# Output projection of a two-layer encoder: four leading first-half products, the gated product kept in PSUM, three residual rows, and the first half's forms in three stages

## The chip, the cores and the metric

The kernel runs on one core of one Trainium2 chip. The metric is the device time of one execution in microseconds (us); the time of a kernel is the median of several runs. The engines are named as in the profile: PE (TensorE, matmuls and transposes), ACT (ScalarE), DVE (VectorE), POOL (GpSimd) and SP (SyncE, which issues all DMA transfers of this kernel). The granted clock is the share of TensorE's full clock that the throttle let through.

## The reference

The reference is one inference step of a streaming encoder with two layers, for 1024 prompt tokens and 128 sample tokens (8 sequences of 16), at a width of 1024. Each layer has an attention mixer and a gated feed-forward block with a short causal convolution. What matters here is the end of the mixer and the start of the feed-forward block:

```
mix = o @ w_o                                    # o: attention output
x = layer_norm(alpha * x + (1 + g_m) * mix, ln_g, ln_b)
h = x * (1 + sc_f) + sh_f                        # affine by c, per group
f, conv_rows = conv_ffn(h, prev, w_up, conv_w, conv_b, w_down)
```

Layer 0 attends over a sliding window, layer 1 over a wider chunk band with a shared key/value projection. All arithmetic is float32. The kernel gets it on PE by splitting each operand into a high part of a shorter format and the low rest: three matmuls (low x high, high x low, high x high) make one product.

## The kernel before, in words

The 1152 tokens are nine tiles of 128; tiles 0 to 7 are the prompt, tile 8 is the sample group. A framework lays the instructions out: the program is traced in Python order, and a planner with its own model of durations then decides, when the kernel is built, in which order each engine issues its instructions. Every engine works its own order off strictly; data dependencies become semaphore waits. `issue_after(ins)` ties the instructions of a block behind a given one on that one's engine. Buffers are columns of a few large SBUF tensors (F with 11040 columns, HX, X1, wh/wl for split weights, ws for raw ones), cut by hand; two uses of the same columns order each other.

`attention` walks through 16 heads (pairs `c`, `a` of chunk and half) with four groups of queries each, and weaves the sample group's items into them. The normalised output of each half head (`normalise`, L709 to 720: c, a and the half h of the tokens) lies in `on` (F columns) and goes to DRAM, from where it is read back chunk by chunk, split, and put into HX (`oload`); the last chunk (c = 7) is split directly into HX, in two halves of 512 tokens. The sample group's output goes through the DRAM tensor oSD.

`out_proj` (L1013) follows, once per layer. It loads the output weights in eight pieces (L1019), four for the first 512 output columns (w0) and four for the last 512 (w1); the places of w1's last two pieces are free only when the attention's last values are done. A product (`half`, L1036; matmuls at L395) is 24 matmuls of 512 columns into one PSUM bank, from a ring of four banks. DVE multiplies it by the gate (L1041) into a temporary in F, and adds ALPHA times the residual row (L1042). After both halves of a tile `norm_tail` (L967) computes the statistics, normalises (L970), lets PE transpose the tile (L976) into banks of a second ring of four, and lets ACT (L988, or DVE at L1005 for the sample tile) apply the affine into a place `hb[HOME[t]]`; the row is stored to xd (L996). The order of the tiles is ORD. The first two and the last two go as pairs (both first halves, then both second halves), the five between one by one. The residual rows (`residual`, L1010) come into a ring of two buffers.

The feed-forward block multiplies 2 x 2 blocks with seven products instead of eight, so it needs seven sums of blocks, here called forms (P1 to P7), of both its operands. `forms` (L1131) makes them for the tokens, in two halves of the tokens (q = 0 and 1), each in three parts i (two tiles' first halves, the sample tile's share, the second halves): three or four subtractions and seven splits (ACT casts at L165, POOL or DVE subtracts at L176). For q = 0 they run on POOL, for q = 1 on DVE. `prep` (L1081) does the same for the weights, on ACT and POOL. `up_phase` (L1171) starts with `unit(0, (0,))` (matmuls at L1196): block 0 of the weights times the first half of the tokens, into banks 0 to 2; its intermediate copies (L1214) and sums (L1217) lie in the columns of F that `out_proj` used.

Around the change, the columns of F hold, before: the sample keys and values of the attention (0 to 2176), `on` (2176 to 3200), sample tables, the block-diagonal queries `qbd` (3744 to 5792); and in `out_proj` the sample gate (0 to 1024), the product's temporary (1024 to 2048), the prompt gate (2048 to 3072), and the two residual buffers (3072 to 5120).

Of the kernel before, what the change touches and what calls it, by code (L numbers as in the profile page):

```python
# [13 lines left out]
ALU = mybir.AluOpType  # L14
# [7 lines left out]
ALPHA = 4.0 ** 0.25  # L22
# [19 lines left out]
ITEMS = [24 + 3 * k for k in range(8)] + [51 + (3 * k) // 2 for k in range(8)]  # L42
VA = ()
BIG = 1e30
ORD = (0, 2, 8, 1, 3, 4, 6, 5, 7)
HOME = {0: 0, 8: 1, 2: 2, 1: 3, 3: 4, 4: 0, 6: 2, 5: 3, 7: 4}
GRP = ((0, 1, 2), (3, 4, 5), (6, 7, 8))
P1, P2, P6, P5, P7, P4, P3 = range(7)
# [6 lines left out]
class Ring:  # L55
# [4 lines left out]
    def next(self):  # L60
        r = self.items[self.i % len(self.items)]
        self.i += 1
        return r
# [30 lines left out]
class Trunk:  # L94
# [361 lines left out]
    def attention(self, l, wk):  # L456
        nc, I = self.nc, self.I
# [23 lines left out]
        fa = Arena(self.F)  # L481
        sKt = fa.take(2176)
        sV = ga.take(1536)
        on = fa.take(1024)
        sb = fa.ring(2, 272)
        sK = Ring([sKt[:, 0:1088], sKt[:, 1088:2176]])
        qbd = fa.take(2048).rearrange("p (c s a q) -> p c s a q", c=8, s=8, a=2)
        pall = fa.take(NP[l] * W)
        pring = Ring([pall[:, i * W : (i + 1) * W] for i in range(NP[l])])
        bias = fa.ring(2, W)  # L490
# [18 lines left out]
        nc.gpsimd.memset(qbd[0:64, :, :, 1, :], 0.0)  # L509
        nc.gpsimd.memset(qbd[64:128, :, :, 0, :], 0.0)  # L510

        def head_of(c, a):
            return 8 * (c // 4) + 4 * a + c % 4 if l == 0 else 2 * c + a
# [19 lines left out]
        else:  # L533
# [8 lines left out]
            qload(0)  # L542
            self.load_hm(Ring([pall[:, i * 1024 : i * 1024 + 1024] for i in range(3)]), self.affine(4, (8, 9), 1))

        if l == 0:
            self.wring = Ring(self.wslots[0:2])
        sbt = []
# [161 lines left out]
        def normalise(c, a, h):  # L709
            r = slice(64 * a, 64 * a + 64)  # L710
            q = slice(h * 512, h * 512 + 512)
            src = self.rD[l][2 * c + a : 2 * c + a + 1, q]
            st = nc.sync.dma_start(rb[r, :], bass.AP(src.tensor, src.offset, [[0, 64], [1, 512]]))
# [300 lines left out]
    def out_proj(self, l, xsrc, xdst, aff):  # L1014
        nc, I, H = self.nc, self.I, self.H
        wo = I[("wo0", "wo1")[l]]
        X1 = self.X1
        loc = ((5120, 6144), (7168, 8192), (0, 2048), (3072, 1024))
        loc = [tuple(X1[:, o : o + 1024] for o in p) for p in loc]  # L1019
        loc = self.wslots[0:2] + loc + [self.wslots[2], (X1[:, 4096:5120], self.wslots[3][1])]  # L1020
        w = [self.wload(wo[i // 4, i % 4], el="ppppvvvv"[i], dst=d) for i, d in enumerate(loc)]
        w0, w1 = w[0:4], w[4:8]
        F = self.F
        self.G = self.x2p.tile([128, 2304], F32R, name=f"gup{l}", tag="x2b")
        self.gateS, tmp, self.gateP = (F[:, i * 1024 : i * 1024 + 1024] for i in range(3))
# [9 lines left out]
        def half(t, x, hf):  # L1035
            ps = self.bank(mb.next())  # L1036
            self.mmX(ps, t * 128, (w0, w1)[hf], 2, 512)
            cs = slice(hf * 512, hf * 512 + 512)
            gate = self.gateP if t < 8 else self.gateS
            v = tr.next()  # L1040
            nc.vector.tensor_mul(v, ps, gate[:, cs])  # L1041
            st = nc.vector.scalar_tensor_tensor(x[:, cs], x[:, cs], ALPHA, v, op0=ALU.mult, op1=ALU.add)  # L1042
            self.lasthalf = st.ins

        def pair(ts, between=None):
            xs = [(t, self.residual(t, xsrc, xring)) for t in ts]
            for t, x in xs:
                half(t, x, 0)
            if between:
                between()  # L1050
            for t, x in xs:
                half(t, x, 1)
                self.norm_tail(t, x, xdst, aff, tb, hb[HOME[t]])

        HX = self.HX
        pair(ORD[0:2])
        for t in ORD[2:7]:
            if t == 8:
                s3 = hb[HOME[8]]
                nc.sync.dma_start(s3, self.oSD.rearrange("c p t -> p c t"))  # L1060
                self.split(s3, H[:, t, 0], H[:, t, 1], "a", "v")
            x = self.residual(t, xsrc, xring)
            half(t, x, 0)
            half(t, x, 1)
            self.norm_tail(t, x, xdst, aff, tb, hb[HOME[t]])
# [11 lines left out]
        pair(ORD[7:], lambda: self.first.extend(self.first.pop()()))  # L1077
        self.fring = Ring(self.fslots[3:8] + [self.fslots[0], self.fslots[8]] + self.fslots[1:3])
        self.late = [self.forms(1, hb, "v", i) for i in range(3)]

    def prep(self, l, j, n=7):  # L1081
        raw = []
# [50 lines left out]
    def forms(self, q, hb, e, i):  # L1133
# [17 lines left out]
        put(P2, b21)  # L1151
        with ExitStack() as es:
            if q:
                es.enter_context(self.tc.issue_after(self.lasthalf))
            put(P3, b22)
            E.tensor_sub(b11, b12, b11)
            E.tensor_sub(b12, b22, b12)
            E.tensor_sub(b22, b22, b11)
            E.tensor_sub(b21, b21, b22)
            put(P6, b22)  # L1160

        def rest():
            put(P5, b11)
            put(P7, b12)
            put(P4, b21)

        return rest

    def ffn(self, l, xsrc, xdst, affs):
        self.up_phase(l)  # L1170
# [2 lines left out]
    def up_phase(self, l):  # L1173
# [112 lines left out]

        unit(0, (0,), self.first)
        for f in self.late:
            f()
        w1 = prep(1)  # L1290
        unit(1, (0,), w1)
        for p in U:
# [317 lines left out]
```

## Time and profile before

| | us |
|---|---|
| runs shown | 2827.95, 2832.05, 2833.47 |
| median | 2832.05 |
| profiled execution | 2830.41 |
| its span, first to last instruction | 2828.6 |
| attention, out_proj and the start of the up phase, layer 0 | about 110 to 545 |
| the same, layer 1 | about 1560 to 2096 |

The mean granted TensorE clock of the profiled execution was 0.986. In the span's 40 slices PE is busy nine tenths in nearly all. Times in the profile are counted from the span's first instruction. A row of a timeline reads: start, duration, engine, line, operation, output<-input, shapes and count, and in square brackets how long the engine stood idle before it and what ended that. A row of stretches reads: start:end, length, busy time with the number of instructions, granted clock, busy share of the DMA engines, GB/s.

### The profile page before, as it was taken

What the parts mean: (1) busy time and instruction counts of PE and PEld (TensorE: products, weight loads), DVE (VectorE), ACT (ScalarE), POOL (GpSimd) and SP (SyncE); (2) the same over time, 40 slices, a digit from 0 to 9 for tenths busy, and PEclk for the clock granted to TensorE, in tenths of its full rate; (3) what the DMA queues carried; (4) which work ended last, traced back from release to release, by engine and by line L of the source; (5) the groups of instructions that cost most, each with busy time, mean ns of one, the idle gap of its engine ahead of it and who ended that gap; (6) DMA issues with size and microseconds to landing.
All of it is one profiled execution on the core that took longest, in us unless ns stands there. A gap on an engine that the chain in (4) does not pass through costs nothing.

```text
span 2828.6 us, 48878 instructions
## 1 busy us (share of the span) xinstructions
PE 2710.7 (96%) x18086; PEld 2423.8 (86%) x18086; DVE 1664.5 (59%) x3830; ACT 1409.2 (50%) x3012; POOL 1064.3 (38%) x1086
## 2 busy tenths in 40 slices
PE   8999889999999999999999999988999999999998
PEld 6987768899999998888998888866799999998886
DVE  4466656755555566766213677774766555567764
ACT  3565644554444444545425666662455545555441
POOL 1122337775566530001541121231877666640000
PEclk9999999999999999999999999999999999999999
DMA  8655343244433447865975457683222222239661
GB/s 327 193 154 170 113 131 116 92 139 140 145 131 132 151 157 266 309 216 183 308 236 183 112 146 188 171 248 99 98 89 79 71 74 81 78 101 296 228 208 72
DMA packets 215870, 454.47 MB, mean 161 GB/s; under 512 B 39280, under 2 KB 115264, under 8 KB 215632
## 3 DMA queue, kind: packets, MB, share of 16 engines
q1 hardware_dynamic: 215632, 451.35, 49.5%
q8 instruction: 143, 2.34, 0.3%
q14 instruction: 95, 0.78, 0.1%
HBM read 359.40 MB, written 101.30 MB: 163 GB/s over the span
## 4 chain that ended last, share of the span: by engine, by line
PE 76%; DMA 7%; DVE 7%; issue 4%; ACT 3%; POOL 3%; SPq 0%; POOLq 0%; DVEq 0%; ACTq 0%
PE PS L1196 33%; PE PS L1347 16%; PE PS L383 11%; PE PS L395 5%; PE PS L679 2%; DMA F<-in_adaw_dram 2%; PE PS L660 2%; PE PS L318 2%; PE PS L634 1%; POOL HX L176 1%; PE PS L637 1%; DVE F L600 1%; DMA ws<-in_wo_dram 1%; ACT HX L165 1%; DMA ws<-oN 1%
## 5 line engine op out<-in xcount | busy, mean ns | idle before, releaser
L176 POOL TENSOR_TENSOR wl<-ws,wh 128x512 fp32r<-128x512 f32 (+1 forms) x217 | 324.5, 1498 | 653.2 <-ACT wh L165 629.5
L1250 DVE SCALAR_TENSOR_TENSOR PS<-F,PS 128x512 f32<-128x512 f32 (+2 forms) x704 | 348.7, 516 | 145.8 <-ACT PS L1257 61.0
L1196 PE MATMUL PS<-HX,wh 128*128 128x288 f32 x2616 | 401.8, 297 | 0.0
L165 ACT CAST wh<-ws 128x512 fp32r<-128x512 f32 (+1 forms) x321 | 244.8, 768 | 315.1 <-PE PS L1347 94.4
L1196 PEld LDWEIGHTS PS<-HX,wh 128*128 128x128 f32 x2616 | 365.2, 189 | 8.1 <-issue 7.4
L1347 PE MATMUL PS<-wh,HX 128*128 128x512 f32 x1164 | 362.1, 390 | 0.8 <-DVE HX L176 0.8
L1196 PE MATMUL PS<-HX,wl 128*128 128x288 f32 x1536 | 254.1, 297 | 7.0 <-DVE F L1217 4.7
L1347 PEld LDWEIGHTS PS<-wh,HX 128*128 128x128 f32 x1164 | 218.5, 188 | 46.0 <-DVE HX L176 1.3
L383 PE MATMUL PS<-HX,wh 128*128 128x384 f32 x1248 | 245.7, 340 | 0.0
L1196 PEld LDWEIGHTS PS<-HX,wl 128*128 128x128 f32 x1536 | 220.0, 189 | 14.4 <-issue 10.4
L1347 PE MATMUL PS<-wl,HX 128*128 128x512 f32 x582 | 226.9, 390 | 0.6 <-DVE wl L176 0.6
L383 PEld LDWEIGHTS PS<-HX,wh 128*128 128x128 f32 x1248 | 217.0, 189 | 5.4 <-issue 2.7
L395 PE MATMUL PS<-wh,HX 128*128 128x256 f32 (+1 forms) x936 | 173.5, 316 | 19.3 <-ACT wh L165 8.8
L1196 PE MATMUL PS<-x1att,wh 128*128 128x288 f32 x1168 | 182.1, 298 | 0.0
L1257 ACT ACTIVATE PS<-F 128x512 f32<-128x512 f32 x176 | 138.1, 785 | 77.5 <-DVE F L1229 63.2
L165 ACT CAST HX<-F 128x384 fp32r<-128x384 f32 (+3 forms) x232 | 135.9, 603 | 68.8 <-PE PS L1347 11.5
L1196 PEld LDWEIGHTS PS<-x1att,wh 128*128 128x128 f32 x1168 | 164.5, 189 | 4.9 <-issue 4.9
L716 POOL TENSOR_TENSOR F<-F,gatt 64x512 f32<-64x512 f32 x62 | 79.5, 1282 | 227.9 <-DVE F L691 201.2
L395 PEld LDWEIGHTS PS<-wh,HX 128*128 128x128 f32 x936 | 137.4, 195 | 30.6 <-ACT wh L165 9.3
L176 DVE TENSOR_TENSOR HX<-F,HX 128x384 fp32r<-128x384 f32 (+2 forms) x188 | 133.5, 719 | 41.3 <-ACT HX L165 40.1
L1347 PE MATMUL PS<-HX 128*128 128x512 f32 x630 | 145.1, 389 | 0.0
L383 PE MATMUL PS<-HX,wl 128*128 128x384 f32 x624 | 130.7, 349 | 9.6 <-DVE HX L167 4.4
(244 smaller groups left out, 5495.8 us busy)
## 6 DMA issues: line engine op xcount, KB each, us to landing
F<-in_adaw_dram SPq DMA_DIRECT2D x112, 512.0 KB
ws<-in_wup_dram SPq DMA_DIRECT2D x92, 512.0 KB
ws<-in_wdn_dram SPq DMA_DIRECT2D x88, 512.0 KB
actD<-F SPq DMA_DIRECT2D x44, 576.0 KB
F<-actD SPq DMA_DIRECT2D x132, 192.0 KB
F<-in_wdn_dram SPq DMA_DIRECT2D x44, 512.0 KB
x1att<-kH SPq DMA_DIRECT2D x60, 256.0 KB
xd<-F SPq DMA_DIRECT2D x27, 512.0 KB
```

The costliest lines, as they stand in the source:

```text
L165: self.lastact = nc.scalar.copy(out, in_).ins
L176: self.eng(el).tensor_sub(lo, src, hi.bitcast(F32))
L318: mm = nc.tensor.matmul(ps[32 * j : 32 * j + 32, hf * 256 : hf * 256 + 256], self.cT[:, k * 32 : k * 32 + 32], w[n][:, j * 256 : j * 256 + ...
L383: self.nc.tensor.matmul(out, w[a][:, k * 128 : k * 128 + 128], self.Hx(p, k, s0, n), start=i == 0, stop=i == 23)
L395: self.nc.tensor.matmul(out[:, 0:n], H[:, t0 // 128, p, j * kn + k, :], w[a][:, k * n : k * n + n], start=i == 0, stop=i == 23,)
L660: nc.tensor.transpose(t[:, m * 128 : m * 128 + 128], p[:, (kt - k0) * 128 : (kt - k0) * 128 + 128], self.ident)
L679: nc.tensor.matmul(ob[:, i0 * 128 : i0 * 128 + w], vst[a][:, kt, :], pp[:, m1 : m1 + w], start=cnt == 0, stop=cnt == 2 * len(order) - 1, s ...
L716: self.eng("v" if last else "p").tensor_mul(on[r, q], on[r, q], rb[r, :])
L1196: nc.tensor.matmul(out, w[f][a][:, k * 128 : k * 128 + 128], x[:, k, :], start=start and i == 0, stop=i == 11, skip_group_check=True,)
L1250: nc.vector.scalar_tensor_tensor(o, v, w(i), o, op0=ALU.mult, op1=ALU.add)
L1257: nc.scalar.activation(yp, u[:, bl, 2:258], AF.Identity, bias=w(3), scale=w(2))
L1347: nc.tensor.matmul(ps, h[p][:, i * 128 : i * 128 + 128], w[q][:, hf * 512 : hf * 512 + 512], start=j == 0 and k == 0, stop=j == NFF - 1 an ...
```

## The change: what it does

- `attention`: in F, `on` moves behind `qbd`, so that `sb` lies at 2176, `qbd` at 2720 and `on` at 4768. The two memsets of `qbd` are traced later, after the key and value projections. The DMA that fetches the reciprocal sums for the half head (7, 1, 0), the last of tokens 0 to 511, is remembered as `earlydma`.
- `out_proj`: the prompt gate lies at 0 to 1024, the sample gate at 4096 to 5120, three residual buffers at 1024 to 4096. The prompt gate and the first three residual rows are issued behind `earlydma`, the sample gate behind the last such DMA, as is the load of the sample tile.
- The order of the tiles is 0, 2, 1, 3, 8, 4, 6, 5, 7 instead of 0, 2, 8, 1, 3, 4, 6, 5, 7. The first-half products of tiles 0, 2, 1 and 3 come first; then each of the four gets its add, its second half and its norm in turn. The last two tiles stay a pair.
- The multiply by the gate writes the product's own PSUM bank, the add reads it there; the temporary is gone. Products have five banks (0 to 4), transposes three (5 to 7).
- `forms` becomes a generator. For q = 0 and two full tiles it has three stages: P1, P3 and three subtractions; P5 and P7; P2, the fourth subtraction, P6 and P4. The first stage of part 0 is traced after the second tile, that of part 2 after the fourth, then the second stage of both; after the sample tile, now the fifth, come its part and all the rest. For q = 1 the operations and their order stay.

The diff, cut to its core:

```diff
-ORD = (0, 2, 8, 1, 3, 4, 6, 5, 7)
+ORD = (0, 2, 1, 3, 8, 4, 6, 5, 7)
...
-        on = fa.take(1024)
         sb = fa.ring(2, 272)
         sK = Ring([sKt[:, 0:1088], sKt[:, 1088:2176]])
         qbd = fa.take(2048).rearrange("p (c s a q) -> p c s a q", c=8, s=8, a=2)
+        on = fa.take(1024)
...
+            if (c, a, h) == (7, 1, 0):
+                self.earlydma = st.ins
...
-        self.gateS, tmp, self.gateP = (F[:, i * 1024 : i * 1024 + 1024] for i in range(3))
-        xring = Ring([F[:, 4096:5120], F[:, 3072:4096]])
+        self.gateP, self.gateS = (F[:, o : o + 1024] for o in (0, 4096))
+        xring = Ring([F[:, i * 1024 : i * 1024 + 1024] for i in (1, 2, 3)])
...
+        with self.tc.issue_after(self.earlydma):
+            self.ln_gate(l, 0, False)
+            xs = [self.residual(t, xsrc, xring) for t in ORD[0:3]]
         with self.tc.issue_after(self.lastdma):
-            self.ln_gate(l, 0, False)
             self.ln_gate(l, 0, True)
-        mb = Ring([0, 1, 2, 3])
-        tb = Ring([4, 5, 6, 7])
-        tr = Ring([tmp[:, 0:512], tmp[:, 512:1024]])
+        mb = Ring([0, 1, 2, 3, 4])
+        tb = Ring([5, 6, 7])
...
-            v = tr.next()
-            nc.vector.tensor_mul(v, ps, gate[:, cs])
-            st = nc.vector.scalar_tensor_tensor(x[:, cs], x[:, cs], ALPHA, v, op0=ALU.mult, op1=ALU.add)
+            nc.vector.tensor_mul(ps, ps, gate[:, cs])
+            st = nc.vector.scalar_tensor_tensor(x[:, cs], x[:, cs], ALPHA, ps, op0=ALU.mult, op1=ALU.add)
...
-        pair(ORD[0:2])
-        for t in ORD[2:7]:
+        ps = [product(t, 0) for t in ORD[0:4]]
+        for n, t in enumerate(ORD[0:4]):
+            x = xs[n] if n < 3 else self.residual(t, xsrc, xring)
+            add(t, x, 0, ps[n])
+            half(t, x, 1)
+            norm(t, x)
+            if n == 1:
+                parts = [self.forms(0, hb, "p", 0)]
+                next(parts[0])
+            elif n == 3:
+                parts.append(self.forms(0, hb, "p", 2))
+                next(parts[1])
+                for f in parts:
+                    next(f)
+        for t in ORD[4:7]:
             if t == 8:
                 s3 = hb[HOME[8]]
-                nc.sync.dma_start(s3, self.oSD.rearrange("c p t -> p c t"))
+                with self.tc.issue_after(self.lastdma):
+                    nc.sync.dma_start(s3, self.oSD.rearrange("c p t -> p c t"))
                 self.split(s3, H[:, t, 0], H[:, t, 1], "a", "v")
...
             if t == 8:
-                rest = [self.forms(0, hb, "p", i) for i in (0, 1)]
-            elif t == 3:
-                rest.append(self.forms(0, hb, "p", 2))
-                for f in rest:
-                    f()
+                parts.append(self.forms(0, hb, "p", 1))
+                next(parts[2])
+                for f in parts:
+                    list(f)
```

More of the change, by code (lines that the diff above doesn't have):

```diff
@@ L507, in attention @@
         kH, kS, vH, vS = self.kH[l], self.kS[l], self.vH[l], self.vS[l]
-        nc.gpsimd.memset(qbd[0:64, :, :, 1, :], 0.0)
-        nc.gpsimd.memset(qbd[64:128, :, :, 0, :], 0.0)
         def head_of(c, a):
@@ L543, in attention @@
             self.load_hm(Ring([pall[:, i * 1024 : i * 1024 + 1024] for i in range(3)]), self.affine(4, (8, 9), 1))
+        nc.gpsimd.memset(qbd[0:64, :, :, 1, :], 0.0)
+        nc.gpsimd.memset(qbd[64:128, :, :, 0, :], 0.0)
         if l == 0:
@@ L1028, in out_proj, with product, add @@
         with self.tc.issue_after(self.lastdma):
-            self.ln_gate(l, 0, False)
             self.ln_gate(l, 0, True)
-        mb = Ring([0, 1, 2, 3])
-        tb = Ring([4, 5, 6, 7])
-        tr = Ring([tmp[:, 0:512], tmp[:, 512:1024]])
-        def half(t, x, hf):
+        mb = Ring([0, 1, 2, 3, 4])
+        tb = Ring([5, 6, 7])
+        def product(t, hf):
             ps = self.bank(mb.next())
             self.mmX(ps, t * 128, (w0, w1)[hf], 2, 512)
+            return ps
+        def add(t, x, hf, ps):
@@ L1038, in half @@
             cs = slice(hf * 512, hf * 512 + 512)
             gate = self.gateP if t < 8 else self.gateS
-            v = tr.next()
-            nc.vector.tensor_mul(v, ps, gate[:, cs])
-            st = nc.vector.scalar_tensor_tensor(x[:, cs], x[:, cs], ALPHA, v, op0=ALU.mult, op1=ALU.add)
+            nc.vector.tensor_mul(ps, ps, gate[:, cs])
+            st = nc.vector.scalar_tensor_tensor(x[:, cs], x[:, cs], ALPHA, ps, op0=ALU.mult, op1=ALU.add)
             self.lasthalf = st.ins
[L1045 to L1053, printed above, removed]
@@ L1055, in out_proj, with half, norm @@
-        HX = self.HX
-        pair(ORD[0:2])
-        for t in ORD[2:7]:
+        def half(t, x, hf):
+            add(t, x, hf, product(t, hf))
+        def norm(t, x):
+            self.norm_tail(t, x, xdst, aff, tb, hb[HOME[t]])
+        HX = self.HX
+        ps = [product(t, 0) for t in ORD[0:4]]
[12 more added lines that the diff above has]
+                    next(f)
@@ L1064, in out_proj @@
             half(t, x, 1)
-            self.norm_tail(t, x, xdst, aff, tb, hb[HOME[t]])
+            norm(t, x)
             if t == 8:
-                rest = [self.forms(0, hb, "p", i) for i in (0, 1)]
-            elif t == 3:
-                rest.append(self.forms(0, hb, "p", 2))
-                for f in rest:
-                    f()
+                parts.append(self.forms(0, hb, "p", 1))
+                next(parts[2])
+                for f in parts:
+                    list(f)
         first = [self.fslots[8], self.fslots[0]]
@@ L1076, in out_proj @@
         self.first = self.prep(l, 0, 5)
-        pair(ORD[7:], lambda: self.first.extend(self.first.pop()()))
+        xs = [(t, self.residual(t, xsrc, xring)) for t in ORD[7:]]
+        for t, x in xs:
+            half(t, x, 0)
+        self.first.extend(self.first.pop()())
+        for t, x in xs:
+            half(t, x, 1)
+            norm(t, x)
         self.fring = Ring(self.fslots[3:8] + [self.fslots[0], self.fslots[8]] + self.fslots[1:3])
         self.late = [self.forms(1, hb, "v", i) for i in range(3)]
+        for f in self.late:
+            next(f)
     def prep(self, l, j, n=7):
@@ L1150, in forms @@
         put(P1, b11)
-        put(P2, b21)
+        if q:
+            put(P2, b21)
         with ExitStack() as es:
@@ L1158, in forms @@
             E.tensor_sub(b22, b22, b11)
+            if q:
+                E.tensor_sub(b21, b21, b22)
+                put(P6, b22)
+        yield
+        if q == 0 and i != 1:
+            put(P5, b11)
+            put(P7, b12)
+            yield
+        if q == 0:
+            put(P2, b21)
             E.tensor_sub(b21, b21, b22)
             put(P6, b22)
-        def rest():
+        if q or i == 1:
             put(P5, b11)
             put(P7, b12)
-            put(P4, b21)
-        return rest
+        put(P4, b21)
     def ffn(self, l, xsrc, xdst, affs):
@@ L1288, in up_phase @@
         for f in self.late:
-            f()
+            list(f)
         w1 = prep(1)
```

## The prediction

> **What bounds the kernel now.** I read the page's first part first: how busy TensorE (PE) is.
>
> ```profile
> span 2828.6 us, 48878 instructions
> PE 2710.7 (96%) x18086; PEld 2423.8 (86%) x18086; DVE 1664.5 (59%) x3830; ACT 1409.2 (50%) x3012; POOL 1064.3 (38%) x1086
> ```
>
> PE is busy 96% of the span, so an edit pays only where PE stands still or runs at a lower granted clock. Next I read the two output projections in stretches (columns: PE busy and its count, granted clock, DMA share, GB/s), cut at the long waits that PE's timeline shows there.
>
> ```profile
> 404.00:417.28 13.28, 8.75 (x25) 0.74 0.53 177
> 417.28:501.65 84.37, 84.27 (x393) 1.00 0.29 101
> 501.65:515.11 13.46, 9.13 (x57) 0.87 0.22 78
> 515.11:530.00 14.89, 13.46 (x97) 1.00 0.21 72
> 1934.15:1952.55 18.40, 8.34 (x25) 0.80 0.48 142
> 1952.55:2039.42 86.87, 85.63 (x392) 0.98 0.28 98
> 2039.42:2053.43 14.01, 7.60 (x57) 1.00 0.19 75
> 2053.43:2068.00 14.57, 14.01 (x91) 0.88 0.19 73
> ```
>
> Rows 2 and 6 are the long middle of the projection in layers 0 and 1: PE has no gap to give there. Rows 1 and 5, the **front**, are what follows the attention; rows 3 and 7, the **seam**, what follows the last product. PE's timeline names the waits:
>
> ```profile
> 406.32 2.07 PE L395 MATMUL PS<-wh,HX 128*128 128x512 f32 x4 [2.36 <-ACT wh L165]
> 417.28 0.73 PE L395 MATMUL PS<-wh,HX 128*128 128x512 f32 x2 [1.81 <-DVE F L1041]
> 457.25 5.77 PE L395 MATMUL PS<-x1att,HX 128*128 128x512 f32 x24
> 462.85 0.63 PE L395 MATMUL PS<-wh,HX 128*128 128x512 f32 x2
> 507.50 1.25 PE L976 MATMUL PS<-C,F 128*128 128x128 f32 x8 [2.78 <-DVE F L970]
> 1939.76 2.08 PE L395 MATMUL PS<-wh,HX 128*128 128x512 f32 x4 [5.60 <-ACT wh L165]
> 1952.55 1.22 PE L395 MATMUL PS<-wh,HX 128*128 128x512 f32 x2 [4.45 <-DVE F L1041]
> 1988.83 1.06 PE L976 MATMUL PS<-C,F 128*128 128x128 f32 x8 [1.24 <-DVE F L970]
> 2045.80 1.06 PE L976 MATMUL PS<-C,F 128*128 128x128 f32 x8 [3.30 <-DVE F L970]
> 2053.43 0.77 PE L1196 MATMUL PS<-HX,wl 128*128 128x288 f32 x4 [3.11 <-DVE F L1217]
> ```
>
> A product is 24 matmuls and four are open (banks 0 to 3). The third row to the fourth gives the full rate: 24 in 5.60 us, 0.233 us each. At the front the first wait is for late weights (w1, the second half's columns), the second for a bank whose product stands there until the gate comes:
>
> ```profile
> 410.50 0.33 SPq L920 DMA_DIRECT2D F<-gd x1
> 404.01 1.04 ACT L165 CAST HX<-F 128x1024 fp32r<-128x1024 f32 x1 [2.60 <-DMA F<-oSD]
> 408.65 1.22 DVE L176 TENSOR_TENSOR wl<-ws,x1att 128x1024 fp32r<-128x1024 f32 x1
> 409.79 0.69 DVE L176 TENSOR_TENSOR HX<-F,HX 128x512 fp32r<-128x512 f32 x1
> 416.53 1.29 DVE L1041 TENSOR_TENSOR F<-PS,F 128x512 f32<-128x512 f32 x2 [6.05 <-DMA F<-gd]
> 1941.63 1.23 DVE L176 TENSOR_TENSOR wl<-ws,x1att 128x1024 fp32r<-128x1024 f32 x1
> ```
>
> ACT stood behind the sample tile's load before it could cast w1; the last low part of w1 was there at 409.87 and 1942.86. The prompt gate could only be loaded at 410.50, when the attention output `on` had been read for the last time (409.79 + 0.69), because both lie in the same columns of F; it took 6.0 us.
>
> **The change part by part.** *Four leading products and a fifth bank.* In the stretch 404.00 to 417.28, 24 matmuls ran; at 0.233 us they are 5.6 us, so 7.7 of 13.28 us are lost, to waits and a halved clock (first row; the second is used below):
>
> ```profile
> 406.00:408.00 2.00, 1.68 (x4) 0.50 0.02 6
> 1907.00:1934.20 27.20, 24.78 (x165) 0.94 0.32 90
> ```
>
> Layer 1 loses 18.40 - 5.6 = 12.8 us, and its middle is 86.87 - 84.37 = 2.5 us longer than layer 0's for the same work, of which 1.24 is the wait of the row at 1988.83 and 1.3 a restart at half clock. The front thus holds 7.7 + 12.8 + 1.3 = 21.8 us. Does the change reach all of it? Before, 72 matmuls could run without the late w1 parts: 2 tiles x 24 with w0, and 2 x 12 with the first two parts of w1. Now it is 4 x 24 + 12 = 108: the four tiles hold tokens 0 to 511, which need nothing of the last half head. The 36 more are 8.4 us of work from 404.0 and 1934.15 on, to 412.4 and 1942.6, and the 12 that then follow on bank 4 need the third part first. So the weights (409.87, 1942.86) are in time even if ACT still stands behind the sample tile. If the planner spends some of the 36 in gaps before, that gap is filled instead: no loss.
>
> [...]
>
> *Gate and three residual rows early.* The prompt gate now lies over the sample keys, free when the last sample scores are done, and is issued behind the half head before the last, and the rows too:
>
> ```profile
> 362.99 0.45 PE L763 MATMUL PS<-F 128*32 128x144 f32 x8
> 393.52 0.42 PE L798 MATMUL PS<-F 16*32 16x128 f32 x8
> 381.24 0.45 SPq L713 DMA_DIRECT2D gatt<-rD x1
> 1901.63 0.45 SPq L713 DMA_DIRECT2D gatt<-rD x1
> ```
>
> In layer 0 the gate can go at about 382 and lands near 388; a row may go from 394 (the last read of the sample's new values). In layer 1 all go behind 1901.6. At 6.0 us a load, the gate and the first row are in by 400 in layer 0 and 1914 in layer 1, the other rows 12 us later; bank 0 is wanted when t0's second product is done, 412.4 + 2.8 = 415. On SP they may stand ahead of the last loads of w_o; the price, if these slip by all four loads (24 us), is a rival below. The sample gate goes last, for tile 8, now fifth, some 40 us later: nothing. DVE gets the first four gated adds earlier: 8 operations of about 0.68 us, 5.4 us, where it idled 6.05 us for the gate. Nothing queued behind them is due before w1, so nothing.
>
> *Product stays in PSUM.* The multiply writes its bank, and the add reads it. The bank is held one add longer; five banks at 5.6 us a product cover that.
>
> ```profile
> L1041 DVE TENSOR_TENSOR F<-PS,F x36: 669/679/694, 416.5 to 2045.6; 128x512 f32<-128x512 f32 x36
> L1042 DVE SCALAR_TENSOR_TENSOR F<-F x36: 670/770/1830, 417.7 to 2046.3; 128x512 f32<-128x512 f32 x36
> ```
>
> No PSUM output of this form is shown, so its multiply lies between 0.67 us (the present one) and 1.8 (the worst add); I take 0.68. DVE has room at 11 us of PE per tile: nothing on the path; at the upper end 18 x 1.1 = 20 us of DVE per layer would still fit outside the seam, and cost it up to 2 us. The add reads PSUM for one operand and should stay near 0.68. [...]
>
> *Order, forms in stages, third residual buffer.* Here the seam's rows (timelines of POOL, SP and DVE, two of the chain):
>
> ```profile
> 487.71 2.99 POOL L176 TENSOR_TENSOR wl<-ws,wh 128x512 fp32r<-128x512 f32 x2
> 491.16 0.37 SPq L1010 DMA_DIRECT2D F<-in_xrow_dram x1
> 496.52 0.69 DVE L1042 SCALAR_TENSOR_TENSOR F<-F 128x512 f32<-128x512 f32 x1 [4.34 <-DMA F<-in_xrow_dram]
> 2024.33 4.74 DMA xd<-F
> 796.49 12.78 PE PS L1196 x96
> ```
>
> The same casts and subtractions run on ACT, DVE and POOL. POOL's first weights for the next phase were ready at 490.7, 11 us before PE's last product (501.65); its first forms now start one tile earlier, so this cover shrinks little as PE comes sooner. The memsets only move behind other POOL work of the attention's start, long before the items that read them: nothing.
>
> Today the last row (tile 7) waits for its buffer's store, behind POOL's weights on SP; DVE waits 4.34 us for it, tile 5's norm slides, and PE stands in order at tile 5's transposes (2.78 and 3.30 us). With three buffers the row is there a tile earlier. In rows 3 and 7 of the stretches PE did 48 unit matmuls (12.78/96 = 0.133 us, 6.4 us) and 8 transposes, 0.85 us (row 2: 84.37 less 336 x 0.2333, over seven tiles): 7.2 us. Lost: 6.2 and 6.8, together 13.0 us. What is late next: the first unit copies to columns 2320 to 2896 of F, which now are tile 5's buffer, so it waits for tile 5's store. Before, DVE went on at 496.52 and reached tile 5's transposes at 507.50, 11.0 us. Tile 5's last product now ends 5.6 us before PE's last; with the same 11.0 and 4.7 for the store the copy could start 10.1 us behind the last product. PE covers P1, P2, P5 (36 x 0.133) and the transposes, 5.6 us, so the wait is 4.5 us at most and 0 at least. I take 1.5, nearer to nothing: the 11.0 us held tile 7's add and forms that now go ahead of it. The seam gives 13.0 - 3.0 = 10.0 us.
>
> **Sum.** 21.8 + 10.0 = 31.8 us. The profiled execution took 2830.4 us (its span 2828.6 and 1.8 around it), so 2798.6; the median of the three runs shown is 1.6 us above it: 2800 us.
>
> **The rivals.**
> (1) *The seam stays as long*: the store of tile 5, or DVE's late forms, take the place of the row. For it: DVE is nearly full there. Against: 4.34 us of DVE waiting goes. Front only: 2832 - 21.8 = 2810.
> (2) *The gate isn't early*: SP's order puts the rows, which wait for the last sample read, or the loads of w_o in the way. If w1 comes 24 us later, at 434, PE stands in layer 0 from 412.4 to 434; it had the same 108 matmuls done at 417.28 + 2.8 = 420.1, so it is 14 us worse there. Layer 1, with 40 us from 1901.6 to 1941.6, still gains its 14.1. If the seam stays long too, that is no change, 2832. Against: SP's order is laid out by readiness, and the DMA queues stand half idle (shares 0.53 and 0.48).
> (3) *Slower: ACT holds the transposes' banks.* They have three banks instead of four; ACT takes casts and affines in one order, and a cast waits for POOL's subtractions:
>
> ```profile
> ACT HX L165 <- POOL F L1158: 3.5, 2, 2.1
> ```
>
> The leading tiles come 6.4 us apart (5.6 and 0.85 of transposes), and a tile needs the bank that the tile before gave first, so it decides from about 3.5 us of ACT waiting per tile. If six tiles a layer each stop PE for 3.5 us, that is 42 us against 31.8: 2842. Against: the longest such wait is 2.1 us.
> (4) *More*: the stretches after the seam held 89 and 83 unit matmuls and 8 transposes, 12.7 and 11.9 us, in 14.89 and 14.57: 4.9 us. With the 3.0 of the store, the 1.24 at 1988.83 and the 2.4 us of gaps from 1907 to 1934 filled as well, 43.3 us: 2789.
>
> **How the numbers follow.** Forecast 0.58, (1) 0.18, (2) 0.07, (3) 0.07, (4) 0.10. The range reaches from just under (4), 2788, past (1) to half the front and no seam, 2832 - 10.9 = 2821, so 2822. Measured here, less than 0.2% (5.7 us) can't be told from no change. Faster: forecast, (1) and (4), 0.86; same: 0.07; slower: 0.07.
>
> **What would show it.** In the profile after: no PE wait over 1 us between the attention's last matmul and the first transposes, granted clock 1.00 there; the gate's load issued before `on` is read; DVE's add never above 0.8 us; the last residual row issued before the product that uses it; PE's first wait behind the last product under 3 us. It is wrong if PE waits at a transpose for ACT, if ACT's copy of the first unit waits many us for a store, or if the front's waits stand with other releasers.

## The result, and the profile after

The kernel after takes 2802.4 us (median of six runs, 2797.2 to 2810.2) against 2829.1 for the kernel before in the same session: ratio 0.9907, 95% interval 0.9896 to 0.9919. Its profiled execution took 2800.65 us, 29.8 less than the one before. The page and PE's stretches, cut as before (columns as in the prediction):

```profile
span 2798.5 us, 48858 instructions
...
PE 2700.2 (96%) x18086; PEld 2415.9 (86%) x18086; DVE 1665.2 (60%) x3830; ACT 1408.9 (50%) x3012; POOL 1056.7 (38%) x1086
```

```profile
406.15:493.01 86.86, 86.26 (x401) 1.00 0.35 117
493.01:501.78 8.77, 6.13 (x46) 1.00 0.35 120
501.78:506.50 4.72, 4.72 (x24) 0.65 0.03 8
...
1921.70:2009.50 87.80, 85.39 (x400) 0.98 0.32 110
2009.50:2018.45 8.95, 5.82 (x45) 1.00 0.14 59
2018.45:2030.40 11.95, 9.13 (x48) 0.71 0.21 66
```

Behind the attention PE now goes straight through the products: the front's lost time is gone (first and fourth row; the fourth keeps one wait, at the first transposes). The seam still loses time in three ways: idle time (second and fifth row), the half clock that follows it (third and sixth: 0.65 and 0.71 on average, 0.50 from 504.0 to 506.5 and from 2021.0 to 2024.0), and more waits after that. PE's timeline after names them:

```profile
1997.50 1.32 PE L977 MATMUL PS<-C,F 128*128 128x128 f32 x8 [2.41 <-DVE F L971]
...
501.78 2.09 PE L1225 MATMUL PS<-HX 128*128 128x288 f32 x12 [2.63 <-ACT F L1243]
...
2018.45 1.13 PE L1225 MATMUL PS<-HX 128*128 128x288 f32 x4 [3.13 <-ACT F L1243]
2021.09 1.33 PE L1225 MATMUL PS<-x1att,wl 128*128 128x288 f32 x4 [1.50 <-ACT x1att L165]
2027.93 1.34 PE L1225 MATMUL PS<-x1att,wh 128*128 128x288 f32 x8 [1.08 <-DVE C L933]
```

Lines have moved: products are still L395, the norm is L971, the transposes L977, the unit's matmuls L1225 and its first copy L1243. The transposes of tile 5, which waited 2.78 and 3.30 us before, are in none of these rows: they no longer stop PE.

To follow the gain I compare four points of PE's timeline in the two traces: the first unit matmul (end of the front), the last one of the up phase, and the projection matmul (L383) with which layer 1 goes on after layer 0's feed-forward block.

| | before | after | gain in the part |
|---|---|---|---|
| layer 0, first unit matmul | 501.65 | 493.01 | 8.6 |
| layer 0, last unit matmul | 1054.60 | 1042.62 | 3.3 |
| layer 1, projection matmul | 1542.99 | 1530.96 | 0.1 |
| layer 1, first unit matmul | 2039.42 | 2009.53 | 17.9 |
| layer 1, last unit matmul | 2544.32 | 2514.70 | -0.3 |
| end of the span | 2828.6 | 2798.5 | 0.5 |

So the fronts, each with the attention ahead of it, gave 26.5 us and the up phases, seams included, 3.1. The total is the predicted one; its two terms are not.

### The profile page after: what moved, and what is told of

The parts are those of the page before. It is cut to its first block, busy times and chain, and to the rows that moved or that the text cites. A ratio compares the mean times of both kernels' runs of the same rounds, so it can differ in the third digit from the quotient of the medians.

```text
span 2798.5 us, 48858 instructions
## 1 busy us (share of the span) xinstructions
PE 2700.2 (96%) x18086; PEld 2415.9 (86%) x18086; DVE 1665.2 (60%) x3830; ACT 1408.9 (50%) x3012; POOL 1056.7 (38%) x1086
## 4 chain that ended last, share of the span: by engine, by line
PE 77%; DVE 8%; DMA 7%; issue 4%; ACT 3%; POOL 1%; SPq 1%; POOLq 0%; ACTq 0%; DVEq 0%
PE PS L1225 34%; PE PS L1376 17%; PE PS L383 9%; PE PS L395 7%; DMA F<-in_adaw_dram 3%; PE PS L678 2%; PE PS L318 2%; PE PS L659 2%; PE PS L633 1%; DMA ws<-in_wo_dram 1%; DVE F L599 1%; PE PS L636 1%; DVE x1att L176 1%; PE PS L977 1%; PE PS L799 1%
## 5 line engine op out<-in xcount | busy, mean ns | idle before, releaser
L1225 PE MATMUL PS<-HX,wh 128*128 128x288 f32 x2616 | 401.0, 297 | 0.0
L1225 PEld LDWEIGHTS PS<-HX,wh 128*128 128x128 f32 x2616 | 364.4, 189 | 8.2 <-issue 8.2
L1225 PE MATMUL PS<-HX,wl 128*128 128x288 f32 x1536 | 254.6, 297 | 0.2 <-ACT F L1254 0.2
L383 PE MATMUL PS<-HX,wh 128*128 128x384 f32 x1248 | 245.9, 340 | 0.0
L1225 PEld LDWEIGHTS PS<-HX,wl 128*128 128x128 f32 x1536 | 220.5, 189 | 7.1 <-issue 5.8
L383 PEld LDWEIGHTS PS<-HX,wh 128*128 128x128 f32 x1248 | 217.3, 189 | 5.4 <-issue 3.1
L1225 PE MATMUL PS<-x1att,wh 128*128 128x288 f32 x1168 | 181.9, 298 | 2.9 <-DVE x1att L176 1.3
L1225 PEld LDWEIGHTS PS<-x1att,wh 128*128 128x128 f32 x1168 | 163.9, 189 | 8.9 <-issue 4.9
L395 PE MATMUL PS<-wh,HX 128*128 128x256 f32 (+1 forms) x936 | 168.4, 310 | 0.8 <-DVE C L599 0.8
L395 PEld LDWEIGHTS PS<-wh,HX 128*128 128x128 f32 x936 | 133.8, 191 | 10.3 <-issue 1.5
L383 PE MATMUL PS<-HX,wl 128*128 128x384 f32 x624 | 130.3, 348 | 10.1 <-DVE HX L167 4.8
```

Source lines behind the costliest of these rows:

```text
L383: self.nc.tensor.matmul(out, w[a][:, k * 128 : k * 128 + 128], self.Hx(p, k, s0, n), start=i == 0, stop=i == 23)
L395: self.nc.tensor.matmul(out[:, 0:n], H[:, t0 // 128, p, j * kn + k, :], w[a][:, k * n : k * n + n], start=i == 0, stop=i == 23,)
L1225: nc.tensor.matmul(out, w[f][a][:, k * 128 : k * 128 + 128], x[:, k, :], start=start and i == 0, stop=i == 11, skip_group_check=True,)
```

## The experiments

Each run is the changed kernel with the edit shown. For the seam I count the 288-column matmuls from the first unit on: from the start of the first to the start of the 336th it would be 46.3 us without loss (335 x 0.133 and twice 0.85 of transposes). The expectations below have 53.1 and 56.7 us for the changed kernel and 46.5 without loss; counted matmul by matmul, the control's are 53.5 and 57.1. "Clock" is the granted clock from 395 to 412 us, the end of layer 0's attention. The medians of the kernel before, run beside each group, lay between 2826.6 and 2830.7 us; the intervals reach 2.5 to 7.5 us to either side, so that a difference of a few us between two of these kernels is not clear of the noise.

| kernel | median us | ratio to before, 95% | stretch, layer 0 / 1 | clock |
|---|---|---|---|---|
| before | 2829.07 | 1 | 57.0 / 57.7 | 0.72 |
| after | 2802.38 | 0.9907 (0.9896 to 0.9919) | 53.8 / 57.2 | 1.00 |
| after, control run | 2799.64 | 0.9898 (0.9872 to 0.9924) | 53.5 / 57.1 | 1.00 |
| gate over `on` | 2817.22 | 0.9973 (0.9954 to 0.9992) | 53.7 / 58.9 | 0.90 |
| two leads, four banks | 2813.81 | 0.9953 (0.9939 to 0.9966) | 54.6 / 54.6 | 0.85 |
| four banks | 2804.92 | 0.9922 (0.9906 to 0.9938) | 55.7 / 56.5 | 0.60 |
| two rows | 2814.60 | 0.9955 (0.9938 to 0.9972) | 54.5 / 60.8 | 0.90 |
| two rows, SBUF temporary | 2827.15 | 0.9997 (0.9988 to 1.0006) | 58.4 / 64.2 | 0.90 |
| forms late | 2799.99 | 0.9903 (0.9885 to 0.9920) | 53.5 / 58.1 | 0.55 |
| other ring order | 2806.17 | 0.9929 (0.9905 to 0.9953) | 51.8 / 57.6 | 0.60 |
| late forms partly on POOL | 2806.89 | 0.9930 (0.9910 to 0.9951) | 55.2 / 59.4 | 0.51 |
| late forms behind the first sum | 2798.95 | 0.9897 (0.9884 to 0.9910) | 49.9 / 56.5 | 1.00 |
| the two edits together | 2800.30 | 0.9908 (0.9894 to 0.9923) | 51.0 / 54.7 | 0.68 |
| no late forms on DVE | 2792.92 | 0.9870 (0.9845 to 0.9895) | 47.7 / 48.5 | 0.60 |

In what follows the leads are the four first-half products that come first, a row is a residual row, and the late forms are those of the second half of the tokens, which DVE makes around the seam. The theory at the start was that what is left of the seam is the wait of the first copy for tile 5's store (A); its rival was that DVE's work holds it, whatever the buffers (B).

**Control.**

> The changed kernel itself, as the control on this chip: about 30 us below the kernel before (ratio near 0.991). Its trace should show the same three waits behind the last product: 2.6 and 3.1 us at the first unit (behind ACT's copy), and about 1.5 and 1.1 us at the second and third groups of layer 1.

It did as expected, with the same waits (2.63 us in layer 0; 3.25, 1.84 and 0.79 in layer 1).

### The front: gate, leads, banks

**Gate over `on`.**

```diff
-        self.gateP, self.gateS = (F[:, o : o + 1024] for o in (0, 4096))
+        self.gateS, self.gateP = (F[:, o : o + 1024] for o in (0, 4096))
...
-            self.ln_gate(l, 0, False)
             xs = [self.residual(t, xsrc, xring) for t in ORD[0:3]]
         with self.tc.issue_after(self.lastdma):
+            self.ln_gate(l, 0, False)
             self.ln_gate(l, 0, True)
```

> The two gates change places: the prompt gate lies over the attention's output rows again, as in the kernel before, and is loaded behind the attention's last transfer; the residual rows are still early, four products still lead. Theory (an early gate is a condition of the front's gain: without it the five banks are full until the gate lands): PE works through 4 x 24 and 12 matmuls, 25 us, and then waits in layer 1 for the gate, loaded behind 1921.9 and landing some 8 to 15 us later, before the tail of attention is over: with the sample gate in its place this costs 2 to 6 us in layer 0 and 5 to 12 in layer 1, 8 to 18 us in all. Rival (five banks and 25 us of products cover the load): within 3 us of the changed kernel.

The median is 17.6 us above the control's, at the upper end of what was expected. Its profiled execution is one of the longest, 15.3 us above its own median, so I read only the mechanism from it; the DVE and PE timelines of that run:

```profile
1939.63 1.90 DVE L1045 TENSOR_TENSOR PS<-PS,F 128x512 f32<-128x512 f32 x3 [6.08 <-DMA F<-gd]
```

```profile
1942.30 1.22 PE L395 MATMUL PS<-x1att,HX 128*128 128x512 f32 x2 [4.50 <-DVE F L1046]
```

DVE waits for the gate, and PE for the bank whose product stands there: before's second wait at the front, back again with five banks and four leads. The early gate is a condition of most of the front's gain.

**Two leads, four banks.**

```diff
-        mb = Ring([0, 1, 2, 3, 4])
-        tb = Ring([5, 6, 7])
+        mb = Ring([0, 1, 2, 3])
+        tb = Ring([4, 5, 6, 7])
...
-        ps = [product(t, 0) for t in ORD[0:4]]
+        ps = [product(t, 0) for t in ORD[0:2]]
...
-            add(t, x, 0, ps[n])
+            add(t, x, 0, ps[n] if n < 2 else product(t, 0))
```

> Two leading products instead of four, and four banks for products and four for transposes as in the kernel before; all else as changed, the early gate and rows too. Theory (the front is filled by first-half columns of four tiles, which need nothing of the last weights): 72 matmuls are to be had without the late weights instead of 108, so PE waits for the last weights again, about 5 us in layer 0 and 8 in layer 1, with some of it at half clock: 11 to 16 us slower than the changed kernel, so more than half of its front gain is lost. Rival (the early gate and rows carry the front): less than 5 us slower.

14.2 us slower: the theory holds. Layer 0's first unit comes 3.5 us later than in the control, and layer 1's front is 8.2 longer. Part of it is a wait for cast weights, 1.23 us at this place in the control; from PE's timeline:

```profile
394.99 1.22 PE L395 MATMUL PS<-x1att,HX 128*128 128x512 f32 x2 [2.67 <-ACT x1att L165]
```

**Four banks** (only the first four lines of that diff).

> Four banks for products and four for transposes as before; four products still lead. Theory (what fills the front are the leads; the fifth bank adds the 12 matmuls that start a second product early): 96 matmuls to be had without the late weights instead of 108, 2.8 us less per layer, of which some was not needed: 0 to 6 us slower than the changed kernel. Rival (banks held through the added in-place product are what limits the front): PE waits behind DVE's add for a bank in each of the first tiles, 8 us or more.

5.3 us slower, inside the expected 0 to 6, but not where it was expected: layer 1's front is 2.4 us shorter than the control's. Layer 0's first unit is 3.2 us later, and that run had the lower clock there (0.60 against 1.00). So the front's loss with two leads is the leads' and not the bank's; what the fifth bank itself is worth stays open within that.

### The rows and the product in PSUM

**Two rows.**

```diff
-        xring = Ring([F[:, i * 1024 : i * 1024 + 1024] for i in (1, 2, 3)])
+        xring = Ring([F[:, i * 1024 : i * 1024 + 1024] for i in (1, 2)])
...
-            xs = [self.residual(t, xsrc, xring) for t in ORD[0:3]]
+            xs = [self.residual(t, xsrc, xring) for t in ORD[0:2]]
...
-            x = xs[n] if n < 3 else self.residual(t, xsrc, xring)
+            x = xs[n] if n < 2 else self.residual(t, xsrc, xring)
```

> Two residual buffers instead of three (the product still stays in PSUM, so the third place is simply not used). The prediction gave the third buffer 10.0 us of seam. Theory after the experiment with the other ring order (the seam is DVE's work, whose start the row only shifts): the row comes late again, DVE waits 2 to 5 us for it, and the seam of each layer is 1 to 4 us longer, 2 to 8 in all, against the changed kernel. Rival (the row has nothing to do with the time any more): within 1.5 us.

15.0 us slower, twice the upper end. In layer 1 the row is late as foreseen, by DVE's timeline of that run:

```profile
2020.31 0.69 DVE L1046 SCALAR_TENSOR_TENSOR F<-F,PS 128x512 f32<-128x512 f32 x1 [5.82 <-DMA F<-xd]
```

The stretch is 1.1 and 3.7 us longer. But layer 0's first unit is also 2.4 us later and layer 1's front 9.1 longer: rows that come late hold banks all through the projection. DVE's groups show it (mean ns of one | idle time before the group, and for what):

```profile
L1046 DVE SCALAR_TENSOR_TENSOR F<-F,PS 128x512 f32<-128x512 f32 x36 | 24.1, 682 | 24.3 <-DMA F<-in_xrow_dram 13.8 <-DMA F<-xd 10.2
```

and the same group after the change, with three rows, and of the kernel before:

```profile
L1046 DVE SCALAR_TENSOR_TENSOR F<-F,PS 128x512 f32<-128x512 f32 x36 | 24.3, 681 | 6.4 <-DMA F<-xd 2.6 <-DMA F<-in_xrow_dram 2.3 <-PE PS L395 1.1
```

```profile
L1042 DVE SCALAR_TENSOR_TENSOR F<-F 128x512 f32<-128x512 f32 x36 | 34.0, 958 | 26.4 <-DMA F<-xd 13.7 <-DMA F<-in_xrow_dram 12.2
```

DVE stood 25.9 us for rows before, 4.9 after, 24.0 with two buffers.

**Two rows, SBUF temporary.** The run before, and the product written to the third buffer's place:

```diff
+        tr = Ring([F[:, 3072:3584], F[:, 3584:4096]])
...
-            nc.vector.tensor_mul(ps, ps, gate[:, cs])
-            st = nc.vector.scalar_tensor_tensor(x[:, cs], x[:, cs], ALPHA, ps, op0=ALU.mult, op1=ALU.add)
+            v = tr.next()
+            nc.vector.tensor_mul(v, ps, gate[:, cs])
+            st = nc.vector.scalar_tensor_tensor(x[:, cs], x[:, cs], ALPHA, v, op0=ALU.mult, op1=ALU.add)
```

> Two residual buffers and the gated product in an SBUF temporary (the third buffer's place), as in the kernel before; all else as changed. Against the run with two buffers and the product in PSUM it shows what the operand in PSUM is worth by itself. Theory (the add with one SBUF operand isn't held by POOL): the add's slowest again reaches 1.8 us where it never exceeded 0.69, its mean rises from 0.69 to about 0.78 us, 36 x 0.09 = 3 us of DVE, most of it beside other work: 0 to 4 us slower than that run. Rival (the bank is free one add earlier, which helps PE at the front): up to 3 us faster.

12.6 us slower than with the product in PSUM, where at most 4 was expected. With early gate, four leads and five banks all in place it is no faster than the kernel before (ratio 0.9997). Its add:

```profile
L1048 DVE SCALAR_TENSOR_TENSOR F<-F 128x512 f32<-128x512 f32 x36 | 37.9, 1071 | 37.4 <-DMA F<-xd 20.2 <-DMA F<-in_xrow_dram 16.8
```

The add takes 1.07 us on average instead of 0.68, 13.8 us over 36 of them, and DVE then waits 37.0 us for rows, whose buffers come free later. In this run the add takes between 0.68 and 1.82 us. In the kernel before, whose add also has both inputs in SBUF, the long ones lie beside POOL: by DVE's and POOL's timelines there, the 11 adds that no POOL operation overlaps take 0.69 us at most, the 24 that POOL overlaps for a third of their time or more 1.09 us on average. With three rows the temporary was not tried.

### The seam: who holds it

**Other ring order.**

```diff
-        xring = Ring([F[:, i * 1024 : i * 1024 + 1024] for i in (1, 2, 3)])
+        xring = Ring([F[:, i * 1024 : i * 1024 + 1024] for i in (2, 1, 3)])
```

> The three residual buffers are handed out in the order second, first, third, so that tile 5's row lies in columns 1024 to 2047 and no longer under columns 2320 to 2896, into which the first unit copies. Theory A (the first copy waits for tile 5's store, which is what is left of the seam): the copy comes right behind the first unit's products, PE's first waits (2.63 and 3.13 us in the changed kernel) go, and the time falls by 3 to 9 us against the changed kernel. Rival B (ACT is held by the late forms, behind DVE's subtractions, and the copy stands behind them whatever its columns): the waits stay within 0.5 us of 2.6 and 3.1, and the time is within 2 us of the changed kernel.

Half of A's mechanism holds: the first copy now comes straight behind the unit's products, in ACT's timeline of this run

```profile
499.14 0.40 ACT L1243 COPY F<-PS 128x288 f32<-128x288 f32 x1 [1.11 <-PE PS L1225]
```

and PE's two waits for it are gone. But the stretch is only 1.6 us shorter in layer 0 and not shorter in layer 1 (57.6 against 57.1), where PE waits 1.82 and 3.24 us for ACT's casts instead. A's gain of 3 to 9 us isn't there: the median is 6.5 us above the control's (the intervals overlap), and the trace puts 3.8 us of that at layer 0's front, in the clock (last section). The mean clock of its four runs is 0.984 to 0.988, that of the control's 0.989 to 0.993. B's waits of 2.6 and 3.1 us aren't there either, so this run decides for neither.

**Late forms partly on POOL.**

```diff
-        self.late = [self.forms(1, hb, "v", i) for i in range(3)]
+        self.late = [self.forms(1, hb, "pvv"[i], i) for i in range(3)]
```

> The second half's forms of tiles 4 and 6 are made on POOL instead of DVE (7 low parts and 4 subtractions, 11 operations of 0.68 us on DVE or 1.3 us on POOL); the other two groups stay on DVE. Theory (what is left of the seam is DVE's own work: in the changed kernel DVE is busy 5.93 of 6 us from 494 to 500 and 5.70 of 6 from 500 to 506): 7.5 us of DVE work leave the seam or the 20 us before it, tile 7's norm and the first sums come earlier, and each layer gains 2 to 4 us, 4 to 8 in all, against the changed kernel. Rival (the seam is the buffer's wait, or the ring of weights on POOL): 14 us more on POOL, which hold back the second unit's weights, and the time is the same or up to 8 us longer.

The time is the rival's: the median is 7.3 us above the control's (the intervals just overlap), the stretches are 1.8 and 2.3 us longer. Of the 5.0 us by which the profiled span is longer, 3.4 lie in the up phases and 2.5 at layer 0's front, where the clock was 0.51. The mechanism is not the rival's: in layer 1's stretch PE waits 0.40 us for POOL, and longest for DVE's norm, by its timeline:

```profile
2027.08 1.97 PE L977 MATMUL PS<-C,F 128*128 128x128 f32 x8 [7.93 <-DVE F L971]
```

In the first 23.6 us of that seam DVE has 30 operations where it had 36 after the change, but is busy 22.3 us against 21.1; POOL is busy 21.9 us against 14.0. DVE's timeline in layer 1:

```profile
2019.94 1.22 DVE L1180 TENSOR_TENSOR F<-F 128x128 f32<-128x128 f32 x1
...
2022.73 0.98 DVE L176 TENSOR_TENSOR x1att<-F,x1att 128x128 fp32r<-128x128 f32 x1
...
2024.31 0.95 DVE L934 TENSOR_TENSOR C<-C 128x1 f32<-128x1 f32 x1
```

The last one is a multiply of one column; after the change it took 0.16 us at 2027.97, as POOL stood idle. So beside the busier POOL the 30 operations keep DVE busy 1.2 us longer than the 36 did: the six that it is spared gain it nothing.

**Late forms behind the first sum.**

```diff
-        for f in self.late:
-            next(f)
...
-                        nc.vector.tensor_add(u0[2 * q], X, ca)
+                        self.sum0 = nc.vector.tensor_add(u0[2 * q], X, ca).ins
...
-        for f in self.late:
-            list(f)
+        with self.tc.issue_after(self.sum0):
+            for f in self.late:
+                list(f)
```

> All of the second half's forms on DVE are issued behind DVE's first sum of the first unit, so that tile 5's and tile 7's norms, the first affines and the first copy and sum stand alone there. Theory (the seam is held by the late forms, which DVE, stretched by POOL, takes in order ahead of tile 7's norm and of the first sum): the first copy and tile 7's transposes come 2 to 4 us earlier, PE's waits and the clock losses in the first 336 unit matmuls (53.1 and 56.7 us in the changed kernel, 46.5 without any loss) shrink by 2 to 4 us per layer, 4 to 8 in all. Rival (the late forms are what PE works on while the first half's units wait, or the same work only moves behind): the stretch to 336 matmuls keeps its length or is up to 4 us longer, and the time is from 2 us below to 8 us above the changed kernel's.

In layer 0 the stretch shrinks by 3.6 us, as foreseen, in layer 1 by only 0.6; there PE now stands for a low part of these forms:

```profile
2021.92 2.29 PE L1223 MATMUL PS<-x1att,wh 128*128 128x288 f32 x8 [5.04 <-DVE x1att L176]
```

The whole time doesn't move measurably (0.9897 against the control's 0.9898). In layer 1 the moved work still comes due in the same 50 us.

**The two edits together.**

> The run before with the other order of the residual buffers as well, so that the first copy waits neither for tile 5's store nor behind the late forms. If both waits hold the seam in turn, it is 1 to 3 us per layer below the run with the late forms alone; if the first copy was never what counts, within 1.5 us of it.

No different from the late forms alone (1.4 us above it, overlapping intervals; stretches 1.2 us longer in layer 0, 1.8 shorter in layer 1): in the time, no gain from freeing the first copy shows.

**No late forms on DVE.**

```diff
+            if q:
+                self.copy("a", hi, src)
+                return
             self.split(src, hi, lo, "a", e)
...
-            E.tensor_sub(b11, b12, b11)
-            E.tensor_sub(b12, b22, b12)
-            E.tensor_sub(b22, b22, b11)
+            if q == 0:
+                E.tensor_sub(b11, b12, b11)
+                E.tensor_sub(b12, b22, b12)
+                E.tensor_sub(b22, b22, b11)
             if q:
-                E.tensor_sub(b21, b21, b22)
                 put(P6, b22)
```

> DVE's part of the second half's forms is left out: 33 operations a layer, the 12 subtractions and the 21 low parts; ACT's casts stay, made from the values that stand there, so what the next phase multiplies is not the reference's. Theory (DVE's queue, with POOL beside it, is the whole of what is left of the seam): the stretch from the first unit to the 336th unit matmul, 53.1 and 56.7 us in the changed kernel, falls to 47 to 50 us in both layers, and the time by 8 to 15 us. Rival (what is left is the chain of product, copy and sum through three banks, tile 5's and tile 7's norms, and POOL's weights): 51 to 55 us, and the time falls by less than 6 us.

The stretch is 47.7 and 48.5 us, close to the loss-free 46.3; in layer 0 no wait of PE over 0.15 us is left in it. All engines in the first 23.5 us of the seams, after the change and then without these operations (PE, PEld, DVE, ACT, POOL busy, clock, DMA share, GB/s):

```profile
493.00:516.50 23.50, 20.86 (x146) 20.30 (x145) 20.27 (x38) 14.78 (x39) 12.20 (x11) 0.93 0.25 90
2009.50:2033.00 23.50, 17.55 (x112) 16.36 (x111) 21.06 (x35) 13.22 (x36) 14.06 (x15) 0.85 0.26 89
```

```profile
494.50:518.00 23.50, 23.50 (x182) 23.50 (x181) 7.16 (x16) 17.34 (x43) 17.28 (x18) 1.00 0.41 128
2008.50:2032.00 23.50, 22.96 (x173) 22.36 (x172) 7.91 (x16) 17.31 (x44) 18.83 (x22) 1.00 0.32 105
```

DVE falls from 20 or 21 us of work to 7 or 8, and PE does 173 to 182 matmuls where it did 112 to 146, with the same copies, store, norms and buffers. For the stretch B is shown. Whether PE waits for the late forms themselves or for what stands behind them in DVE's queue, this run doesn't separate: it leaves out both. The up phases are 5.6 and 9.3 us shorter than in the control; the profiled span falls by less, 10.8 us, since this run's fronts are 0.9 and 3.6 us longer. The medians differ by 6.7 us, less than the 8 to 15 foreseen, and their intervals overlap, so the worth for the whole kernel isn't settled.

**Forms late.** All first-half forms after the fifth tile:

```diff
-            if n == 1:
-                parts = [self.forms(0, hb, "p", 0)]
-                next(parts[0])
-            elif n == 3:
...
-                parts.append(self.forms(0, hb, "p", 1))
-                next(parts[2])
+                parts = [self.forms(0, hb, "p", i) for i in (0, 2, 1)]
+                for f in parts:
+                    next(f)
                 for f in parts:
                     list(f)
```

> The first half's forms are all made after the fifth tile (tile 8) instead of in three stages around it; nothing else changes. Theory (the stages were there to keep POOL clear of the first weights of the next phase): POOL does the same 33 operations some 12 us later, the weights' forms on POOL come late by as much, and the first units wait: 4 to 10 us per layer, 8 to 20 in all, against the changed kernel. Rival (POOL had 11 us of cover, as the prediction counted it, and PE's front is what counts): within 3 us.

The theory fell: no difference in time (2799.99 against 2799.64), the stretch unchanged in layer 0 and 1.0 us longer in layer 1. The three stages aren't what made the kernel faster.

## Why the prediction was right, and where its terms were not

**Right in sum.** 2800.0 was predicted, 2802.4 measured, and 2800.65 in the profiled execution against 2798.6. That the sum came so close is luck: the front gave 4.7 us more than its term and the seam 6.9 less. The leads and the early gate do what the steps say. The gate is issued as foreseen, and the last row well ahead of its use (SP's timeline after):

```profile
1887.88 0.58 SPq L921 DMA_DIRECT2D F<-gd  x1
...
472.87 0.33 SPq L1011 DMA_DIRECT2D F<-in_xrow_dram  x1
```

The add never takes more than 0.69 us, no PE wait over 1 us is left between the attention's last matmul and the first transposes, and the clock there is 1.00. One sign failed: PE's first wait behind the last product, to be under 3 us, was 3.13 in layer 1.

**Front: 21.8 predicted, 26.5 measured.** The step that was too small is "Does the change reach all of it?", which counted the leads as work for the two waits only and left the "2.4 us of gaps from 1907 to 1934" to a rival. PE's end of layer 1's attention, from the first product to the attention's last matmul, before and after:

```profile
1896.40:1934.15 37.75, 31.05 (x217) 0.95 0.39 113
```

```profile
1885.80:1932.60 46.80, 45.56 (x290) 1.00 0.46 135
```

Before, 72 product matmuls ran in that time and 6.7 us were idle; after, 145 ran and 1.2 us were idle. The planner spent the leads, and second halves behind them, in the tail's gaps as well. That is the excess: layer 1 gave 17.9 us against the 14.1 counted for it (12.8 and 1.3). Layer 0 gave 8.6 against 7.7, and only with the full clock: with the forms late, the other ring order or some late forms on POOL, where the clock was 0.51 to 0.60, its first unit starts at 496.07 to 498.49, a gain of 3.2 to 5.6. The whole front can't be given to the leads, though: without the third row 11.5 us of it are lost, and with the temporary as well 18.0, by the first units of those runs against the control's. Both steps had been priced at "nothing on the path" outside the seam.

**Seam: 10.0 predicted, 3.1 measured** (3.8 by the stretch to the 336th matmul). The step that failed is "I take 1.5, nearer to nothing: the 11.0 us held tile 7's add and forms that now go ahead of it". The row's wait did go, and tile 5's transposes with it; but the forms that "go ahead" are the very thing that stands in the way. ACT's and DVE's timelines after, layer 1:

```profile
2015.89 0.82 ACT L165 CAST HX<-F 128x512 fp32r<-128x512 f32 x2 [5.44 <-DVE F L1178]
2016.61 1.50 ACT L989 ACTIVATE F<-PS,C 128x128 f32<-128x128 f32 x4
2018.00 0.41 ACT L1243 COPY F<-PS 128x288 f32<-128x288 f32 x1
```

```profile
2012.47 1.68 DVE L176 TENSOR_TENSOR x1att<-F,x1att 128x512 fp32r<-128x512 f32 x1
2014.08 1.78 DVE L1178 TENSOR_TENSOR F<-F 128x512 f32<-128x512 f32 x1
...
2017.05 2.02 DVE L1179 TENSOR_TENSOR F<-F 128x512 f32<-128x512 f32 x2
```

ACT waits 5.44 us for DVE's late subtraction, then does tile 5's affine, then the copy that PE waits for. The price of one wait was also taken for the price of the seam: the prediction closed its account 13.5 and 14.0 us behind the last product, while the stretch to the 336th matmul loses 22.2 us over both layers before and 18.4 after, half-clock time included. Of these 18.4, all but 3.7 go with DVE's late forms. So rival (1), which named them, was right about the mechanism; at 2810 it missed the time by the front's excess and the seam's 3.1 us.

**PSUM operand.** The multiply into PSUM was taken at 0.68 us and took 0.69. Its worth was taken as nothing outside the seam; in the pair with two rows it was 12.6 us. In that pair the add took 1.07 us on average with both inputs in SBUF and 0.68 with one of them in PSUM. After the change, too, 24 of the 36 adds are overlapped by POOL for a third of their time or more, and none of those takes more than 0.69 us.

## What to carry to other kernels

An engine that is 60% busy over the span can still be the whole bound of a 25 us stretch (DVE after the change: 20.3 and 21.1 us busy of 23.5): read its busy time there before pricing a wait, because a wait taken from a full queue gives back only what the queue leaves open (here 3.1 us of the 10.0 counted). Work that PE can do without the late input (here, first columns of four tiles) is worth more than the wait it is meant for, since it also fills the gaps before (26.5 us against 21.8). And edits that each cost "nothing" can hold each other up: with two rows and an SBUF temporary the fronts still gain 8.1 us over the kernel before, but the up phases lose 8.0, and the leads, the early gate and the fifth bank bring nothing in sum.

## What the hardware showed that was not expected

Behind nearly the same waits of PE the granted clock fell to 0.50 in one run and stayed at 1.00 in another. The run with the other ring order has the control's PE order up to the seam of layer 0, and waits of 1.31 and 0.53 us where the control has 1.23 and 0.52. PE's stretches, first of that run, then of the control:

```profile
392.00:396.00 4.00, 3.59 (x21) 1.00 0.39 131
396.00:400.00 4.00, 2.58 (x6) 0.75 0.16 52
400.00:404.00 4.00, 3.45 (x27) 0.50 0.27 97
```

```profile
392.00:396.00 4.00, 4.00 (x23) 1.00 0.57 187
396.00:400.00 4.00, 2.25 (x9) 1.00 0.14 10
400.00:404.00 4.00, 3.02 (x32) 1.00 0.65 208
```

The one falls to 0.50, the other stays at 1.00, and the first unit starts 3.8 us later (497.36 against 493.58). The kernel with the forms late shows what this may do to a comparison: its profiled execution, with 0.55 in that place, took 2805.3 us, its other three 2798.9 to 2800.6; the mean clock of those is 0.990 to 0.993 against 0.987, and 17 us at 0.50 would make 0.003 of it, but where they lost clock isn't recorded. What decides between the two clocks stays open.
